# Array halves used in pairs, four pairs of weight halves for ten raw chunks: one change to a hybrid attention, scan and expert block

## The chip, the cores and the metric

The kernel runs on one core of one Trainium2 chip. The metric is the device time of one execution in microseconds; the kernel of before was run three times. An execution was also recorded by the hardware profiler, and every time that is shown here comes from the runs or from this record. In it PE is TensorE (matmul), PEld its weight loads, DVE VectorE, ACT ScalarE, POOL GpSimd and SP SyncE, which issues the weight transfers. L185 is line 185 of the kernel.

## The reference

512 tokens of width 1024 go through one block: modulation by a condition, a joint in-projection, attention in which an index score keeps 128 keys for each query, a Mamba2 scan beside it, a gated mix, and then 32 experts of which each token takes four.

```python
h = _rms(x, norm_mix[l]) * (1.0 + sc_m) + sh_m
q, kv_lat, q_i, k_i, w_i, z, xbc, dt_raw, gate_logits = _split(h @ w_in[l])
...
dots = jnp.einsum('bqhd,bsd->bqhs', qib, k_idx)              # index scores, 8 heads of 64
score = jnp.einsum('bqh,bqhs->bqs', wib, jax.nn.relu(dots))
_, sel = lax.top_k(score, topk)                              # 128 keys of a query
logits = jnp.einsum('bqhd,bqkhd->bqhk', qb, kg) * scale + bias   # 8 heads of 64
...
wmat = cb[..., None] * lmat * dtc[:, None]                   # scan: 16 heads of 64, chunks of 128
y = jnp.einsum('bijgh,bjghp->bighp', wmat, xc)
y = y + jnp.einsum('bign,bghpn->bighp', cc, state) * jnp.exp(acum)[..., None]
...
mixed = jax.nn.sigmoid(g_attn) * y_attn + jax.nn.sigmoid(g_ssd) * y_ssd
x = x + g_m * (mixed @ w_out[l])
h = _rms(x, norm_ffn[l]) * (1.0 + sc_f) + sh_f
...
gu = xb @ w_gu[e] + b_gu[e]                                  # expert e, blocks of 128 tokens
g, u = jnp.minimum(gu[:, :D_EXPERT], 7), jnp.clip(gu[:, D_EXPERT:], -7, 7)
out = ((u + 1.0) * (g * jax.nn.sigmoid(1.702 * g))) @ w_dn[e] + b_dn[e]
```

## The kernel before

**Weights.** Every weight chunk of 1 MB is loaded raw by SP's queue (`load` L176, `mload` L926) and split in two halves in the engine's rounded float type: the high half is a copy by ScalarE (`whi` L184, `mhi` L1297), the low half the rest, by VectorE (`wlo` L185, `mlo` L1298). TensorE then does three products, activations' high half by both and their low half by the weights' high half (L392 to L394 before the experts, L1338 to L1340 in them). In the experts a chunk is 12 matmuls of 128x512, and an expert is 12 chunks: four for gate and up (`gu`), two for down (`dn`), twice. The raw chunks go round a ring of buffers, RAW2 + 2 + RAW + RAW3 = 6 + 2 + 2 + 1 = 11; the halves go round HI + HI2 = 2 + 1 = 3 pairs (`msplit` L1283). A chunk's pair is asked for by `refill` (L1308) each time that `weights` hands one out, and EARLY = 3 of them are split before the first expert.

**Experts.** For gate and up, `gated` (L1267) lets ScalarE write silu into `g`, `upped` (L1271, L1272) has VectorE clip up into `u` and multiply into `act`. The activations are transposed on TensorE and split into `ah` (ScalarE, L1257) and `al` (VectorE, L1262), tokens likewise into `xh` and `xl` (L1259). `y` (L1368) is VectorE's eviction of `dn` with the gate. `si` (L1236) are the rows to which a block's result is scattered, and `put` (L1275) scatters it with a DMA. A scheduler decides the final order of each engine; it is pinned, so that an instruction that waits holds up all behind it.

**Before the experts.** A string, ORDER, says in which order the in-projection's pieces are written: c0 to c5 are the convolution's chunks, s1a to s3b index scores of four heads at 256, 384 and 512 keys (`scores`, L478), m is a piece of the modulation that VectorE computes. Then `weave` (L261) merges three stages by position: the scan with gate chunks and the top-128 search; attention with the z part; and the rest. In the scan, `ssd_terms` makes a head's two matrices (TensorE L752, L753, L759; then ScalarE's exponentials and VectorE's products), and `ssd_sum` adds up its output (L773, L775), one head at a time in 64 of the array's columns. In attention, `att_logits` makes one head's logits (L817, from 64 rows) and adds the mask (L818), VectorE adds a bias (L821), ScalarE takes the exponential; `att_sum` (L833 on) transposes and multiplies by the values.

Of the kernel before, what the change touches and what calls it, by code (L numbers as in the profile page):

```python
# [22 lines left out]
P = 128  # L23
# [110 lines left out]
def program(tc, A, dbg=None, upto=99):  # L134
# [5 lines left out]
    with ctx:  # L140
# [49 lines left out]
        RAW, HI, LO, RAW2, RAW3, HI2, R2, RAWP, EARLY = 2, 2, 2, 6, 1, 1, 6, 1, 3  # L190
        NS, ZEND, LATE, XFIRST = (4, 25, (0, 2, 3, 2.5), True)
# [9 lines left out]
        ORDER = "L S s1a R s1b m m s2a LT c0 K0 k0 m K1 VT c1 s2b m k1 Q0 c2 m c3 q0 s3a Q1 q1 s3b m m c4 m c5 m"  # L201
# [5 lines left out]
        with ExitStack() as c1:  # L207
# [264 lines left out]
            def scores(qt, hs):  # L472
                n = (qt + 1) * P
                sc = score[:, qt - 1, 0:n]
                for h in hs:
                    r = slice((h % 2) * 64, (h % 2) * 64 + 64)
                    p = pt("at")
                    T.matmul(p[:, 0:n], qiT[r, h // 2, qt * P:(qt + 1) * P], kiT[r, 0:n], start=True, stop=True)  # L478
                    rl = r2()
                    S.activation(rl[:, 0:n], p[:, 0:n], AF.Relu, scale=0.125)  # L480
                    if h == 0:
                        V.tensor_scalar(sc, rl[:, 0:n], wi8[:, qt, h:h + 1], None, op0=OP.mult)
                    else:
                        V.scalar_tensor_tensor(sc, rl[:, 0:n], wi8[:, qt, h:h + 1], sc, op0=OP.mult, op1=OP.add)
# [6 lines left out]
            dt_ = con.tile([P, NT, 16], F32, name="dt")  # L491
            acum, dec, expt = (con.tile([P, NT, 16], F32, name=n_) for n_ in ("acum", "dec", "expt"))
            hlt = []

            def steps():
# [185 lines left out]
            def vals():  # L681
                for t in range(NT):
# [10 lines left out]
                        s1a=lambda: scores(1, range(0, 4)), s1b=lambda: scores(1, range(4, 8)),  # L693
                        s2a=lambda: scores(2, range(0, 4)), s2b=lambda: scores(2, range(4, 8)),
                        s3a=lambda: scores(3, range(0, 4)), s3b=lambda: scores(3, range(4, 8)))
# [5 lines left out]
            bt, cT, hl = later["bt"], later["cT"], hlt[0]  # L701

# [44 lines left out]
            def ssd_terms(h):  # L747

                g = h // 8
                sel = selr[0:64, h:h + 1].to_broadcast([64, P])  # L750
# [3 lines left out]
                lm = r2((P, NT, P))  # L754
# [5 lines left out]
                ca = r2((P, 3 * P))  # L760
# [4 lines left out]
            def ssd_sum(h):  # L765
                g, a = h // 8, h % 2
                lm, ca = terms.pop(h)
                if a == 0:
                    terms["y"] = pt("sy")
                yp = terms["y"]  # L770
                for c in range(NT):
                    o = yp[a * 64:(a + 1) * 64, c * P:(c + 1) * P]
                    T.matmul(o, xdt[:, c, h * 64:(h + 1) * 64], lm[:, c, :], start=True, stop=(c == 0))  # L773
                    if c:
                        T.matmul(o, sts[:, slot[g][c - 1], (h % 8) * 64:(h % 8 + 1) * 64], ca[:, (c - 1) * P:c * P],  # L775
                                 start=False, stop=True)
                if a:
                    i = h // 2
                    V.scalar_tensor_tensor(yD[:, i, :], yD[:, i, :], dskip[:, i:i + 1], yp, op0=OP.mult, op1=OP.add)
# [15 lines left out]
            for g in range(2):  # L795
                scan += [lambda g=g, c=c: state(g, c) for c in range(3)]
                scan.append(lambda g=g: inner(g))
                for h in range(8 * g, 8 * g + 9):
                    scan += [lambda h=h: ssd_terms(h)] * (h < 8 * g + 8) + [lambda h=h: ssd_sum(h - 1)] * (h > 8 * g)
# [11 lines left out]
            def att_logits(qt, h):  # L811
                n = (qt + 1) * P
                if h == 0:
                    atts[qt] = pt("ac"), sm([P, 8], name="den")
                r = slice((h % 2) * 64, (h % 2) * 64 + 64)
                p = pt("at")
                T.matmul(p[:, 0:n], qT[r, h // 2, qt * P:(qt + 1) * P], kT[r, h // 2, 0:n], start=True, stop=False)  # L817
# [770 lines left out]
```

## Time and profile before

| what | value |
| --- | --- |
| time, median of 3 runs (range) | 1861.55 us (1860.41 to 1867.49) |
| time of the profiled execution, its span | 1862.16 us, 1860.3 us |
| TensorE busy, matmuls | 1783.4 us (96%), x8652 |
| VectorE busy | 1540.1 us (83%) |
| ScalarE busy | 1076.5 us (58%) |
| DMA, mean | 283 GB/s |

The span is the profiled time from the first instruction to the last. The shares are means over stages that differ: the parts before the experts take some 630 us, the experts the rest.

### The profile page before, as it was taken

The numbers are of one execution on the slowest core, as the hardware profiler recorded it, in microseconds if no ns is written. First come the engines' busy times: TensorE is split into PE (matmuls) and PEld (weight loads), VectorE is DVE, ScalarE is ACT, GpSimd is POOL, SyncE is SP. The second block draws the span as 40 slices with busy tenths as digits, with TensorE's granted clock in tenths as the row PEclk, the third lists the DMA queues.
The fourth block names the chain that finished last, engine by engine and source line by source line (L and its number), as shares of the span: only waits on it lengthen the run. The fifth ranks groups of instructions, "written<-read, shape, count | busy, mean of one in ns | idle before, by whom it ended". The sixth has DMA issues, their size and how long they took to land. (4 is left out here: it accounts for less than half of the span.)

```text
span 1860.3 us, 22834 instructions
## 1 busy us (share of the span) xinstructions
PE 1783.4 (96%) x8652; PEld 1400.4 (75%) x8652; DVE 1540.1 (83%) x1891; ACT 1076.5 (58%) x1059; POOL 191.9 (10%) x114
## 2 busy tenths in 40 slices
PE   7998999999999798999999999999999999999996
PEld 3777777776678577888888877777777777777875
DVE  6586787764776788999999899989899989988986
ACT  4453432344423365777777776766676667666764
POOL 0000000000000111101101101201111111210201
PEclk9999999999899799999999999999999999999998
DMA  8232343421575589999999999999999999999992
GB/s 324 91 139 89 114 161 123 144 105 69 187 264 210 198 276 352 371 369 369 390 375 374 365 363 373 361 367 355 382 358 347 384 381 340 361 384 354 369 345 56
DMA packets 86456, 527.26 MB, mean 283 GB/s; under 512 B 10912, under 2 KB 11072, under 8 KB 32072
## 3 DMA queue, kind: packets, MB, share of 16 engines
q1 hardware_dynamic: 70552, 469.70, 65.7%
q0 software_dynamic: 15552, 55.97, 11.1%
q8 instruction: 69, 1.13, 0.2%
q14 instruction: 43, 0.35, 0.1%
q10 hardware_dynamic: 240, 0.10, 0.0%
HBM read 497.91 MB, written 30.45 MB: 284 GB/s over the span
## 5 line engine op out<-in xcount | busy, mean ns | idle before, releaser
L185 DVE TENSOR_TENSOR wlo<-raw,whi 128x2048 fp32r<-128x2048 f32 x242 | 551.7, 2285 | 63.7 <-ACT whi L184 61.1
L184 ACT ACTIVATE whi<-raw 128x2048 fp32r<-128x2048 f32 x242 | 463.7, 1917 | 173.8 <-PE mm L393 73.4
L1297 ACT ACTIVATE mhi<-raw 128x2048 fp32r<-128x2048 f32 x104 | 199.7, 1921 | 86.4 <-PE gu L1340 74.0
L1298 DVE TENSOR_TENSOR mlo<-raw,mhi 128x2048 fp32r<-128x2048 f32 x104 | 237.4, 2283 | 1.8 <-ACT mhi L1297 1.8
L1339 PE MATMUL gu<-wlo,xh 128*128 128x512 f32 x520 | 209.4, 403 | 11.5 <-DVE wlo L185 11.4
L1339 PE MATMUL dn<-wlo,ah 128*128 128x512 f32 x508 | 205.3, 404 | 6.4 <-DVE wlo L185 5.4
L1338 PE MATMUL gu<-whi,xh 128*128 128x512 f32 x520 | 206.5, 397 | 0.0
L1340 PE MATMUL gu<-whi,xl 128*128 128x512 f32 x520 | 206.3, 397 | 0.0
L1340 PE MATMUL dn<-whi,al 128*128 128x512 f32 x508 | 201.2, 396 | 0.0
L1338 PE MATMUL dn<-whi,ah 128*128 128x512 f32 x508 | 199.7, 393 | 0.0
L1338 PE MATMUL gu<-mhi,xh 128*128 128x512 f32 x504 | 197.9, 393 | 1.4 <-ACT mhi L1297 1.4
L1339 PE MATMUL gu<-mlo,xh 128*128 128x512 f32 x504 | 198.3, 394 | 0.4 <-DVE mlo L1298 0.4
L1340 PE MATMUL gu<-mhi,xl 128*128 128x512 f32 x504 | 197.6, 392 | 0.0
L1275 POOL DMA_INDIRECT out_dram<-y,si x31 | 96.9, 3127 | 849.3 <-DVE y L1368 824.8
L393 PE MATMUL mm<-B,whi 128*128 128x512 f32 x352 | 140.1, 398 | 0.0
L392 PE MATMUL mm<-bA,whi 128*128 128x512 f32 x320 | 132.1, 413 | 3.8 <-ACT whi L184 1.8
L394 PE MATMUL mm<-bA,wlo 128*128 128x512 f32 x320 | 128.8, 404 | 4.2 <-DVE wlo L185 4.2
L1339 PEld LDWEIGHTS gu<-wlo,xh 128*128 128x128 f32 x520 | 98.0, 188 | 41.2 <-DVE wlo L185 21.6
L1339 PEld LDWEIGHTS dn<-wlo,ah 128*128 128x128 f32 x508 | 96.3, 190 | 35.8 <-DVE wlo L185 14.0
L1338 PEld LDWEIGHTS gu<-whi,xh 128*128 128x128 f32 x520 | 98.1, 189 | 22.0 <-ACT xh L1257 0.2
L1340 PEld LDWEIGHTS gu<-whi,xl 128*128 128x128 f32 x520 | 98.0, 188 | 20.8 <-DVE xl L1259 0.2
L1339 PEld LDWEIGHTS gu<-mlo,xh 128*128 128x128 f32 x504 | 95.0, 188 | 23.5 <-DVE mlo L1298 2.6
(453 smaller groups left out, 3122.7 us busy)
## 6 DMA issues: line engine op xcount, KB each, us to landing
raw<-in_w_gu_dram SPq DMA_DIRECT2D x209, 1024.0 KB
raw<-in_w_dn_dram SPq DMA_DIRECT2D x105, 1024.0 KB
B<-in_w_gu_dram SPq DMA_DIRECT2D x47, 1024.0 KB
raw<-in_w_in_dram SPq DMA_DIRECT2D x23, 1024.0 KB
B<-in_w_dn_dram SPq DMA_DIRECT2D x23, 1024.0 KB
rawp<-in_w_ada_dram POOLq DMA_DIRECT2D x30, 512.0 KB, 4.2
bE<-in_w_ada_dram SPq DMA_DIRECT2D x4, 1024.0 KB
bC<-in_x_dram SPq DMA_DIRECT2D x8, 512.0 KB
```

What stands on the lines that cost most here:

```text
L184: S.activation(hi[:, 0:n], raw[:, 0:n], AF.Copy)
L185: i = V.tensor_tensor(lo[:, 0:n], raw[:, 0:n], hi[:, 0:n].bitcast(F32), op=OP.subtract)
L392: T.matmul(p, wh, xT[0][:, k, :], start=(k == 0), stop=False)
L393: T.matmul(p, wh, xT[1][:, k, :], start=False, stop=False)
L394: T.matmul(p, wl, xT[0][:, k, :], start=False, stop=(k == nk - 1))
L1275: G.indirect_dma_start(out=out, out_offset=bass.IndirectOffsetOnAxis(ap=si, axis=0), in_=y, in_offset=None, compute_op=OP.add)
L1297: S.activation(hi, raw, AF.Copy)
L1298: i = V.tensor_tensor(lo, raw, hi.bitcast(F32), op=OP.subtract)
L1338: T.matmul(p, x[0][:, kk, :], hi[:, ws], start=(b is None and kk == 0), stop=False)
L1339: T.matmul(p, x[0][:, kk, :], lo[:, ws], start=False, stop=False)
L1340: T.matmul(p, x[1][:, kk, :], hi[:, ws], start=False, stop=(kk == KD - 1))
```

## The change

Index scores, logits, scan sums and attention sums are written for two heads at a time: both heads' matmuls stand next to each other in the code, each in its half of the array, and the steps that follow come behind. ORDER spreads the scores as pairs (s10 is the pair of heads 0 and 1 at 256 keys). The selector and `hl` of `ssd_terms` are widened from 64 to 128 rows, the new ones zero. The scan's and attention's temporaries get buffers of their own (`te`, six) beside `r2`. In the experts there are two pairs `mhi`/`mlo` (HI2 = 2), four pairs in all, and the eleventh raw chunk (`raw3`) goes; EARLY is 4; and ScalarE writes the gate straight into `act`, so `g` goes.

```diff
-        RAW, HI, LO, RAW2, RAW3, HI2, R2, RAWP, EARLY = 2, 2, 2, 6, 1, 1, 6, 1, 3
-        NS, ZEND, LATE, XFIRST = (4, 25, (0, 2, 3, 2.5), True)
+        RAW, HI, LO, RAW2, HI2, R2, RAWP, EARLY = 2, 2, 2, 6, 2, 6, 1, 4
+        NS, ZEND, LATE, XFIRST = (4, 13, (0, 2, 3, 2.5), True)
...
-        ORDER = "L S s1a R s1b m m s2a LT c0 K0 k0 m K1 VT c1 s2b m k1 Q0 c2 m c3 q0 s3a Q1 q1 s3b m m c4 m c5 m"
+        ORDER = "L S s10 R s12 m s14 m s16 LT s20 c0 s22 K0 k0 s24 m K1 VT s26 c1 m k1 s30 Q0 s32 c2 m s34 c3 q0 s36 Q1 q1 m m c4 m c5 m"
...
-                for h in hs:
-                    r = slice((h % 2) * 64, (h % 2) * 64 + 64)
-                    p = pt("at")
+                pair = [(h, slice((h % 2) * 64, (h % 2) * 64 + 64), pt("at")) for h in hs]
+                for h, r, p in pair:
                     T.matmul(p[:, 0:n], qiT[r, h // 2, qt * P:(qt + 1) * P], kiT[r, 0:n], start=True, stop=True)
+                for h, r, p in pair:
                     rl = r2()
...
-                hl = big("S8", [64, L], F32R)
+                hl = big("S8", [P, L], F32R)
                 hlt.append(hl)
-                S.activation(hl, pw[0:64, :], AF.Copy)
+                V.memset(hl[64:P].bitcast(F32), 0.0)
+                S.activation(hl[0:64], pw[0:64, :], AF.Copy)
...
-                sel = selr[0:64, h:h + 1].to_broadcast([64, P])
+                sel = selr[:, h:h + 1].to_broadcast([P, P])
...
-            def ssd_sum(h):
-                g, a = h // 8, h % 2
-                lm, ca = terms.pop(h)
-                if a == 0:
-                    terms["y"] = pt("sy")
-                yp = terms["y"]
+            def ssd_sum(i):
+
+                g = i // 4
+                two_ = [(h, slice((h % 2) * 64, (h % 2) * 64 + 64), *terms.pop(h)) for h in (2 * i, 2 * i + 1)]
+                yp = pt("sy")
                 for c in range(NT):
-                    o = yp[a * 64:(a + 1) * 64, c * P:(c + 1) * P]
-                    T.matmul(o, xdt[:, c, h * 64:(h + 1) * 64], lm[:, c, :], start=True, stop=(c == 0))
-                    if c:
-                        T.matmul(o, sts[:, slot[g][c - 1], (h % 8) * 64:(h % 8 + 1) * 64], ca[:, (c - 1) * P:c * P],
-                                 start=False, stop=True)
...
+                    cs = slice(c * P, (c + 1) * P)
+                    for h, r, lm, ca in two_:
+                        T.matmul(yp[r, cs], xdt[:, c, h * 64:(h + 1) * 64], lm[:, c, :], start=True, stop=(c == 0))
+                    for h, r, lm, ca in two_ if c else ():
+                        T.matmul(yp[r, cs], sts[:, slot[g][c - 1], (h % 8) * 64:(h % 8 + 1) * 64],
+                                 ca[:, (c - 1) * P:c * P], start=False, stop=True)
...
+                pair = [(h, slice((h % 2) * 64, (h % 2) * 64 + 64), pt("at")) for h in (h0, h0 + 1)]
+                for h, r, p in pair:
+                    T.matmul(p[:, 0:n], qT[r, h // 2, qt * P:(qt + 1) * P], kT[r, h // 2, 0:n], start=True, stop=False)
+                for h, r, p in pair:
+                    T.matmul(p[:, 0:n], identb, mask[:, qt - 1, 0:n] if qt else cmb, start=False, stop=True)
+                for h, r, p in pair:
+                    weighed(qt, h, n, p)
...
-                i = turn[0] % (RAW2 + 2 + RAW + RAW3)
+                i = turn[0] % (RAW2 + 2 + RAW)
...
-            def gated(g, p):
-                S.activation(g, p, AF.Silu, scale=ALPHA)
-
-            def upped(u, p, g, act):
+            def gated(act, p):
+                S.activation(act, p, AF.Silu, scale=ALPHA)
+
+            def upped(u, p, act):
 
                 V.tensor_scalar(u, p, 8.0, -6.0, op0=OP.min, op1=OP.max)
-                V.scalar_tensor_tensor(act, g, SILU7, u, op0=OP.min, op1=OP.mult)
+                V.scalar_tensor_tensor(act, act, SILU7, u, op0=OP.min, op1=OP.mult)
```

Where instructions come to stand is decided by the scheduler. On TensorE in the scan, the first head terms and sums of one group read before as follows (`ss` is a PSUM tile of the terms, `sy` the sums' one; `r_2152` and `r_2160` are one head's two matrices, and rows that read alike are counted behind the x).

```order
L752 MATMUL ss<-cmt,identb 128x512
L753 MATMUL ss<-bS_758,selr 128x512
L759 MATMUL ss<-bS_758,selr 128x384
L773 MATMUL sy<-r_2152,bC 64x128 x2
L775 MATMUL sy<-r_2160,bV 64x128
L773 MATMUL sy<-r_2152,bC 64x128
L775 MATMUL sy<-r_2160,bV 64x128
L773 MATMUL sy<-r_2152,bC 64x128
L775 MATMUL sy<-r_2160,bV 64x128
```

The same place in the changed kernel, where a sum begins behind a head's terms:

```order
L755 MATMUL ss<-cmt,identb 128x512
L756 MATMUL ss<-bS_758,selr 128x512
L762 MATMUL ss<-bS_758,selr 128x384
L776 MATMUL sy<-te,bC 64x128 x4
L778 MATMUL sy<-te,bV 64x128 x2
L776 MATMUL sy<-te,bC 64x128 x2
L778 MATMUL sy<-te,bV 64x128 x2
L776 MATMUL sy<-te,bC 64x128 x2
L778 MATMUL sy<-te,bV 64x128 x2
```

Seven groups of one head have become seven steps in which two heads alternate; a `sy` row counts both.

On VectorE in an expert of the later half (about the eighteenth), before:

```order
L1298 TENSOR_TENSOR mlo<-raw_9639,mhi 128x2048
L185 TENSOR_TENSOR wlo<-raw_9657,whi 128x2048
L1271 TENSOR_SCALAR u<-gu 128x512
L1272 SCALAR_TENSOR_TENSOR act<-g,u 128x512
L185 TENSOR_TENSOR wlo<-raw_9707,whi 128x2048
L1298 TENSOR_TENSOR mlo<-B_9725,mhi 128x2048
L1368 SCALAR_TENSOR_TENSOR y<-dn,gate,gf 128x512
L1262 SCALAR_TENSOR_TENSOR al<-tr,ah 128x512
L185 TENSOR_TENSOR wlo<-B_9746,whi 128x2048
L185 TENSOR_TENSOR wlo<-raw,whi 128x2048
L1298 TENSOR_TENSOR mlo<-raw,mhi 128x2048
L185 TENSOR_TENSOR wlo<-raw_9803,whi 128x2048
```

And the same stretch of the changed kernel:

```order
L1307 TENSOR_TENSOR mlo<-raw,mhi 128x2048
L185 TENSOR_TENSOR wlo<-raw_9680,whi 128x2048
L1280 TENSOR_SCALAR u<-gu 128x512
L1281 SCALAR_TENSOR_TENSOR act<-act,u 128x512
L185 TENSOR_TENSOR wlo<-raw_9698,whi 128x2048
L1307 TENSOR_TENSOR mlo<-raw_9719,mhi 128x2048
L1376 SCALAR_TENSOR_TENSOR y<-dn,gate,gf 128x512
L1271 SCALAR_TENSOR_TENSOR al<-tr,ah 128x512
L1307 TENSOR_TENSOR mlo<-raw_9737,mhi 128x2048
L185 TENSOR_TENSOR wlo<-raw_9758,whi 128x2048
L185 TENSOR_TENSOR wlo<-raw_9776,whi 128x2048
L1307 TENSOR_TENSOR mlo<-B_9808,mhi 128x2048
```

Between the splits, `u`, `act`, `y` and `al` stand where they stood; which splits are `wlo` and which `mlo` is now two and two in turn.

On VectorE at the start of the experts, ahead of the third place that writes `si`, before:

```order
L1467 TENSOR_TENSOR cum<-few 128x24
L1262 SCALAR_TENSOR_TENSOR al<-tr,ah 128x512
L1243 TENSOR_TENSOR gate<-q 128x4
L1466 COPY few<-cum 128x32
L1298 TENSOR_TENSOR mlo<-raw_5884,mhi 128x2048
L1244 TENSOR_TENSOR gate<-gate,q 128x4
L1467 TENSOR_TENSOR cum<-few 128x16
L185 TENSOR_TENSOR wlo<-raw_5902,whi 128x2048
L1236 TENSOR_TENSOR si<-q 128x4
L1468 CAST nbt<-cum 128x1
```

And in the changed kernel:

```order
L1376 SCALAR_TENSOR_TENSOR y<-dn,gate,gf 128x512
L1473 TENSOR_TENSOR cum<-few 128x24
L1271 SCALAR_TENSOR_TENSOR al<-tr,ah 128x512
L1252 TENSOR_TENSOR gate<-q 128x4
L1472 COPY few<-cum 128x32
L185 TENSOR_TENSOR wlo<-raw_5969,whi 128x2048
L1253 TENSOR_TENSOR gate<-gate,q 128x4
L1473 TENSOR_TENSOR cum<-few 128x16
L185 TENSOR_TENSOR wlo<-raw_5987,whi 128x2048
L1245 TENSOR_TENSOR si<-q 128x4
L1474 CAST nbt<-cum 128x1
```

Counted from the first expert on, one split more stands ahead of this `si` now.

## Rows read from the trace of the kernel before

**Rows 1.** Busy time by stretch: per engine us and instructions, TensorE clock, DMA share, GB/s.
```profile
245.00:377.00 132.00, 131.98 (x643) 95.37 (x641) 101.49 (x221) 47.55 (x105) 4.77 (x9) 1.00 0.41 147
245.00:265.00 20.00, 20.00 (x94) 13.66 (x93) 18.66 (x46) 9.70 (x24) 1.59 (x3) 1.00 0.47 165
377.00:448.00 71.00, 70.34 (x346) 50.04 (x345) 41.91 (x121) 31.23 (x82) 2.12 (x4) 1.00 0.22 75
762.00:1104.00 342.00, 342.00 (x1620) 278.92 (x1619) 318.26 (x233) 245.68 (x171) 46.32 (x19) 1.00 1.00 373
1104.00:1820.00 716.00, 703.93 (x3271) 562.47 (x3270) 648.70 (x480) 496.98 (x343) 99.45 (x36) 1.00 0.98 363
```

**Rows 2.** Waits from 1100 to 1800: who waited for whom, us, times, longest.
```profile
DVE u L1271 <- PE gu L1340: 33.5, 34, 1.0
...
DVE wlo L185 <- ACT whi L184: 14.3, 15, 1.0
...
PE gu L1339 <- DVE wlo L185: 10.1, 18, 0.7
...
SPq L942 <- DVE wlo L185: 356.4, 118, 4.2
SPq L942 <- DVE mlo L1298: 117.9, 59, 3.1
```

**Rows 3.** Timeline of VectorE and TensorE in one late expert: start, us, instruction.
```profile
1257.40 0.75 DVE L1368 SCALAR_TENSOR_TENSOR y<-dn,gate,gf 128x512 f32<-128x512 f32 x1 [0.69 <-PE dn L1340]
...
1258.66 4.48 DVE L185 TENSOR_TENSOR wlo<-raw,whi 128x2048 fp32r<-128x2048 f32 x2
...
1261.00 0.50 PE L1339 MATMUL gu<-wlo,xh 128*128 128x512 f32 x1 [0.66 <-DVE wlo L185]
```

**Rows 4.** Timeline of TensorE in the scan.
```profile
257.10 0.39 PE L752 MATMUL ss<-cmt,identb 128*128 128x512 bf16 x1
...
258.02 0.65 PE L773 MATMUL sy<-r,bC 128*64 128x128 f32 x4
...
259.70 0.50 PE L392 MATMUL mm<-bA,whi 128*128 128x512 f32 x1
260.03 0.39 PE L393 MATMUL mm<-B,whi 128*128 128x512 f32 x1
260.26 0.39 PE L394 MATMUL mm<-bA,wlo 128*128 128x512 f32 x1
...
297.90 0.65 PE L773 MATMUL sy<-r,bC 128*64 128x128 f32 x4
...
299.63 0.50 PE L392 MATMUL mm<-bA,whi 128*128 128x512 f32 x1
```

**Rows 5.** Timeline of TensorE, index scores of one and of two heads.
```profile
81.80 0.70 PE L478 MATMUL at<-bK,bV 64*128 64x256 f32 x4
...
88.12 0.70 PE L478 MATMUL at<-bK,bV 64*128 64x256 f32 x2
...
192.42 1.61 PE L478 MATMUL at<-bK,bV 64*128 64x512 f32 x4
...
199.90 1.12 PE L478 MATMUL at<-bK,bV 64*128 64x512 f32 x2
```

**Rows 6.** Timeline of TensorE, logits of one head.
```profile
423.33 0.91 PE L817 MATMUL at<-bE 64*128 64x384 f32 x2
424.18 0.34 PE L818 MATMUL at<-mask,identb 128*128 128x384 bf16 x1
```

**Rows 7.** Timeline of VectorE and TensorE at the start of the experts.
```profile
737.06 0.16 DVE L1236 TENSOR_TENSOR si<-q 128x4 int32<-128x4 f32 x1 [5.98 <-DMA out_dram<-y,si]
...
739.54 0.79 PE L1339 MATMUL dn<-wlo,ah 128*128 128x512 f32 x1 [4.85 <-DVE wlo L185]
```

**Rows 8.** Timeline of TensorE in the in-projection.
```profile
156.53 0.80 PE L394 MATMUL mm<-bA,wlo 128*128 128x512 f32 x1 [4.24 <-DVE wlo L185]
```

**Rows 9.** Waits from 762 to 1100.
```profile
ACT whi L184 <- DMA raw<-in_w_gu_dram: 4.9, 6, 0.9
```

More of the change, by code (lines that the diff above doesn't have):

```diff
@@ L490, in program @@
             na = con.tile([P, 16], F32, name="na")
[L491 to L492 removed]
+            dt_ = W.tile([P, NT, 16], F32, name="dt")
+            acum, dec, expt = (W.tile([P, NT, 16], F32, name=n_) for n_ in ("acum", "dec", "expt"))
             hlt = []
@@ L692, in program @@
                         q0=lambda: head_T(env["Q0"], 0, 0), q1=lambda: head_T(env["Q1"], 0, 2), m=mod_step,
-                        s1a=lambda: scores(1, range(0, 4)), s1b=lambda: scores(1, range(4, 8)),
-                        s2a=lambda: scores(2, range(0, 4)), s2b=lambda: scores(2, range(4, 8)),
-                        s3a=lambda: scores(3, range(0, 4)), s3b=lambda: scores(3, range(4, 8)))
+                        )
+            acts.update({f"s{qt}{h}": lambda qt=qt, h=h: scores(qt, (h, h + 1)) for qt in range(1, NT) for h in range(0, 8, 2)})
             acts.update({f"c{i}": lambda i=i: conv(i) for i in range(6)})
@@ L797, in program @@
                 scan.append(lambda g=g: inner(g))
-                for h in range(8 * g, 8 * g + 9):
-                    scan += [lambda h=h: ssd_terms(h)] * (h < 8 * g + 8) + [lambda h=h: ssd_sum(h - 1)] * (h > 8 * g)
+                for h in range(8 * g, 8 * g + 8):
+                    scan.append(lambda h=h: ssd_terms(h))
+                    if h % 2 == 0 and h > 8 * g:
+                        scan.append(lambda h=h: ssd_sum(h // 2 - 1))
+                scan.append(lambda g=g: ssd_sum(4 * g + 3))
             tops = [lambda qt=qt, i=i: top8(qt, i) for qt in range(1, NT) for i in range(16)]
@@ L896, in program @@
             yhi = big("C", [P, KD, L], F32R)
-            heads_ = [(qt, h) for qt in range(NT) for h in range(8)]
+            heads_ = [(qt, h) for qt in range(NT) for h in range(0, 8, 2)]
             steps_ = []
             for i in range(len(heads_) + 1):
-                steps_.append(lambda i=i: (att_logits(*heads_[i]) if i < len(heads_) else None, att_sum(*heads_[i - 1]) if i else None))
+                steps_.append(lambda i=i: (att_logits(*heads_[i]) if i < len(heads_) else None,
+                                           att_sum(*heads_[i - 1]) if i else None))
             zs = [lambda j=j, b=b: z_part(j, b) for j in range(4) for b in range(2)]
@@ L923, in program, with mload @@
             turn = [0, 0]
-            ahead, side = [], []
-            def mload(queue=nc.sync, tile_=None):
+            ahead = []
+            def mload():
                 src = next(order, None)
@@ L936, in mload @@
                         pool, name, n = M1, "raw2", RAW2
-                    elif i < RAW2 + 2:
+                    else:
                         pool, name, n = WB, f"B{i - RAW2}", 1
-                    else:
-                        pool, name, n = side[0], "raw3", RAW3
-                    raw = tile_ or pool.tile([P, 2048], F32, name=name, tag=name, bufs=n)
-                    i = queue.dma_start(raw, src)
-                    if queue is G:
-                        tc.keep_in_program_order(i)
+                    raw = pool.tile([P, 2048], F32, name=name, tag=name, bufs=n)
+                    nc.sync.dma_start(raw, src)
                 ahead.append(raw)
@@ L1435, in program @@
                     if e < NE:
-                        g, u = mt([P, 512], name="g", bufs=1), mt([P, 512], name="u", bufs=1)
-                        gated(g, three(xT, bias["b_gu"], e, f * 512, "gu", 3))
+                        u = mt([P, 512], name="u", bufs=1)
+                        gated(act[:, fs], three(xT, bias["b_gu"], e, f * 512, "gu", 3))
                         if e + f == 0:
@@ L1444, in program @@
                             held.extend("no")
-                        upped(u, three(xT, bias["b_gu"], e, FE + f * 512, "gu", 3), g, act[:, fs])
+                        upped(u, three(xT, bias["b_gu"], e, FE + f * 512, "gu", 3), act[:, fs])
                         if last:
```

58 lines of the change are left out of this document (28 added, 30 removed).

## The prediction

> **What bounds the kernel now.** I read the summary by engine first, then a table of busy times by stretch, then the waits of the engine that binds, and last the single instructions where the diff works. TensorE binds: in four of the five stretches of [rows 1] it is busy for practically the whole time, so that in them a microsecond taken off TensorE is a microsecond off the span as long as the other engines keep up. VectorE is close behind: 101.49 of 132 us in the stretch of the scan (245 to 377), 18.66 of 20 at its beginning, 318.26 of 342 in the early experts. That is the margin against which every gain below has to hold.
>
> The expert stage is in two regimes. In 762 to 1104 TensorE issues 1620 matmuls in 342 us, 4.737 per us; in 1104 to 1820 it issues 3271 in 716 us, 4.568 per us [rows 1]. At the first rate the second stretch would take 3271 / 4.737 = 690.5 us, so 25.5 us are lost there. [Rows 2] say on what: TensorE waits for wlo, the low half that VectorE makes of a weight chunk, and VectorE waits 33.5 us, 34 times, for TensorE to finish the group that `u` reads. Instructions show how one causes the other [rows 3]: VectorE stands at `y` until TensorE has finished dn, then does `y` and `al`, and only at 1258.66 begins the next low half; TensorE's first matmul with it starts at 1261.00. The pinned order lets VectorE be only one split ahead when it meets `y` or `u`; these two instructions and a split (1.26 us from 1257.40 to 1258.66, then half of the 4.48 us of two splits) take 3.5 us, longer than the 2.7 us for which TensorE can use the chunk it holds (12 matmuls at 0.23, the step of [rows 4] between 260.03 and 260.26). Transfers bind nothing here: the queue that issues them waits 356.4 + 117.9 us of this 700 us for VectorE to release a raw buffer [rows 2].
>
> **The change, part by part.** The sum is made against the profiled execution's own 1862.2 us (span 1860.3); the median of the runs is 1861.55, 0.6 less, which I neglect.
>
> *Index scores (L478).* A head fills half the rows of the array. Two heads on different halves take 0.70 us in 81.80, as long as a lone head in 88.12; at 512 columns a lone head takes 1.12 in 199.90 and a pair whose second head came late 1.61 in 192.42 [rows 5]. The step to the next matmul is some 0.07 shorter than such a row (0.85 against 0.91 in [rows 6]), so 0.63 and 1.05. In the order before, 18 heads stand in pairs and 6 alone, two of each length; now 4 pairs at 256 columns, 3 pairs and 2 lone heads at 384, and at 512 two pairs, three heads in a row and one alone. Fewer clusters: 5 x 0.63 becomes 4 x 0.63 at 256, nothing at 384, between 0 and 0.5 at 512, together 0.6 to 1.1. Lateness like that of 192.42 (0.5 us) is in several pairs of before, and the new code asks for both results before the first matmul. I take 2 us, from 0.6 to 4.
>
> *Scan sums (now L776, L778).* A head uses 64 of the array's columns. Alone it takes 1.68 us for its 14 matmuls (258.02 to 259.70). From 297.90, 18 matmuls take 1.73: four of the next head's stand among the last of the first and cost 0.05 us [rows 4]. If each of the 16 heads ran beside another, 8 x 1.68 = 13.4 us would go. The order shows that the new sums do stand interleaved, two by two. But it breaks 5 of the 8 pairs after the first group or two, and the pieces pay entry and exit. From 0 to 13, I take 8: below the full overlap, above half of it.
>
> *Scan terms.* The three matmuls with the 64-row selector take 0.92 us from 257.10 to 258.02. At the 0.23 of a full step, with 3/4 of it for the third, they would be 0.63 [rows 4]. The selector now has all 128 rows, so a head can lose 0.29 and 16 heads 4.6 us. I take 4.5, since both bounds lie near each other; the zeros for it cost one small memset.
>
> Together 12.5 us of TensorE in the scan. It does not all reach the span: with it gone, VectorE would have 101.49 us of work in 119.5, and in 245 to 265, where it had 1.34 us free, TensorE can't gain more than that. I count nine tenths, **-11**, with 0 and -17 as ends.
>
> *Attention logits (L821).* Before, no two heads' products stood together. One at 384 columns takes 0.85 us (423.33 to 424.18) [rows 6]; the score rows give 0.63 at 256 and 1.05 at 512, and the step between them 0.42 at 128. In the new order 2 of 4 pairs stand together at 128, all 4 at 256, 3 at 384 and only 1 at 512: 0.84 + 2.52 + 2.55 + 1.05 = 7.0 us. TensorE is busy 70.34 of 71 us in the larger part of this stage [rows 1]; the 512-column heads partly lie behind it, where it waits anyway. I take **-6**, from -2 to -9.
>
> *Fourth pair of halves, in steady experts.* This is the largest question: 25.5 us could come back. The order says not. From the twelfth expert on, `u`, `act`, `y` and `al` stand at the same places between splits as before (the steady expert shown above), and VectorE again meets `u` and `y` with one split in hand. A free pair doesn't help an engine whose next instruction is pinned behind `y`. ScalarE may make high halves earlier, but the time lost is in VectorE's queue. I take 0, with -25 as the bound. In experts 2 to 9 VectorE is now one split further ahead, but TensorE lost nothing there. The order falls back to one split ahead some one and a half experts sooner: 25.5 us over 19 experts is 1.3 each, so **+2**.
>
> *Start of the experts.* Writing `si` makes VectorE wait 5.98 us for a transfer, and TensorE stands until 739.54, 4.85 us, for the split behind it [rows 7]. In the new order one more split stands ahead of `si`: 12 matmuls, 2.7 us, with which TensorE fills this wait. Its first steps afterwards are long (0.79 us for the first), and a shorter stop may spare some of them. I take **-3**, from 0 to -5.
>
> *Everything else.* One raw buffer fewer costs nothing while the transfers wait for VectorE, as they do for over two thirds of the time in [rows 2]. The gate written into act's place removes a buffer, no instruction. The stall before 156.53 (4.24 us behind a chain of small norms on VectorE) [rows 8] goes, since its split now stands ahead of the chain, but the split after it has moved behind; I take 0, from -4 to +4. The tail keeps its order.
>
> Sum: -2 -11 -6 +0 +2 -3 = -20, so 1862.2 - 20 = **1842 us**; with the terms' own bounds, not all at once at their ends, 1828 to 1853.
>
> **The rivals.** *B, the fourth pair heals the experts.* If VectorE's waits for ScalarE's high halves, 14.3 us in 15 [rows 2], are what keeps it from getting ahead, a pair more would remove them, and the later experts would run at the early rate: -25, so 1817 us. Against it: the same single split of lead in the pinned order. For it: the early experts, on the same number of pairs, do run with more lead.
>
> *C, TensorE's gain in phase 1 is not realised.* Paired sums ask VectorE and ScalarE for two heads' terms at once. VectorE at 18.66 of 20 us can't deliver faster, and TensorE would then wait for `lm` and `ca`. Scan and attention together would give 4 instead of 17: 1862.2 - 2 - 4 + 2 - 3 = 1855 us. In the worst case, with nothing from either, 1859. The Trainium skill (TensorEngine Tiling (Array Packing), section PSUM Bottleneck) says just this of packing: the array gets faster, evacuating PSUM doesn't, and the copy may become the limit. By that rule the sum would be C's; the trace agrees for the first 20 us of the scan and, with VectorE at 77% of 245 to 377, not for the whole.
>
> *D, ten raw chunks are too few* (slower). A raw buffer is held from the issue of its transfer to the end of its split. A chunk is 12 matmuls, at least 12 / 4.568 = 2.6 us [rows 1], so eleven buffers give each 29 us for this and ten 26. Where issue, landing and split need more than those 26 us, the transfers set the pace. If they needed the full 29, the 1058 us of experts from 762 to 1820 would grow by a tenth, +106, and with the -19 of phase 1 the time would be about 1949; from a fifth of that on, the kernel is slower than before. For it: the DMA share of 1.00 and 0.98 [rows 1], and ScalarE's six waits for a transfer in the early experts, 4.9 us in all [rows 9]. Against it: these waits reach no matmul, no engine waits for a weight transfer later, and the issuing queue itself waits for a buffer over two thirds of the time [rows 2].
>
> **How the numbers follow.** 0.5% of this kernel, about 9.3 us, is what a measurement can tell from no change. Forecast 0.63 (1828 to 1853), B 0.10 (1817), C 0.19 (1853 to 1859), D 0.05 (above 1872), other 0.03. Faster: 0.61 of the forecast, B, and 0.07 of C, 0.78. Same: 0.02 + 0.11 of C + 0.02 = 0.15; slower: D and part of the rest, 0.07. A range from 1816 to 1860 takes in B and C and leaves out D and what lies beyond.
>
> **What would show it.** The scan and attention stretch: TensorE's sums in pairs, 28 matmuls in about 1.7 to 2.2 us, terms in 0.65 us, and the experts' first matmuls some 18 us earlier. In the later experts the same 10 us of TensorE waits for wlo and the same rate of 4.57 matmuls per us. `si` with a TensorE wait of some 2 us instead of 4.85. I would be wrong if the later experts run at 4.7 (B), if TensorE waits in 245 to 377 for `te` (C), or if ScalarE waits for raw transfers (D).

## The result and the profile after

The changed kernel takes **1845.99 us** (median of 5 runs, 1842.02 to 1848.25) against 1861.55 (5 runs, 1859.01 to 1867.49): ratio 0.9911, interval 0.9888 to 0.9933. The forecast was 1842, with a range of 1816 to 1860. The execution that was profiled is the slowest of the five (1848.25 us, span 1846.5), so sums made from its rows come out 2 us short of the medians.

Where did the time go? The simplest way to see it is a ledger of landmarks: instructions that both kernels have once, at the borders of the stages, and the difference of their starts. First the timeline of TensorE in the kernel before: the scan's first state, its last term, the router, the first expert matmul, then the 37th, 145th and 373rd weight chunk of the experts (in experts 3, 12 and 31 of 0 to 31), and the last matmul.

```profile
237.62 0.59 PE L729 MATMUL ss<-r,bF 128*128 128x512 f32 x1
...
368.00 0.44 PE L759 MATMUL ss<-bS,selr 64*128 64x384 f32 x1
...
592.48 0.19 PE L1170 MATMUL mm<-bfc,bK 128*32 128x1 f32 x1
...
646.90 0.79 PE L1338 MATMUL gu<-whi,xh 128*128 128x512 f32 x1
...
774.23 0.39 PE L1338 MATMUL dn<-whi,ah 128*128 128x512 f32 x1
...
1100.97 0.39 PE L1338 MATMUL dn<-whi,ah 128*128 128x512 f32 x1
...
1811.07 0.39 PE L1338 MATMUL dn<-whi,ah 128*128 128x512 f32 x1
...
1847.01 0.40 PE L1340 MATMUL dn<-whi,al 128*128 128x512 f32 x1
```

The same eight in the changed kernel:

```profile
245.25 0.59 PE L732 MATMUL ss<-r,bF 128*128 128x512 f32 x1
...
360.40 0.38 PE L762 MATMUL ss<-bS,selr 128*128 128x384 f32 x1
...
577.58 0.19 PE L1179 MATMUL mm<-bfc,bK 128*32 128x1 f32 x1
...
631.13 0.79 PE L1346 MATMUL gu<-whi,xh 128*128 128x512 f32 x1
...
754.79 0.39 PE L1346 MATMUL dn<-whi,ah 128*128 128x512 f32 x1
...
1083.77 0.39 PE L1346 MATMUL dn<-whi,ah 128*128 128x512 f32 x1
...
1797.10 0.39 PE L1346 MATMUL dn<-whi,ah 128*128 128x512 f32 x1
...
1833.69 0.40 PE L1348 MATMUL dn<-whi,al 128*128 128x512 f32 x1
```

The differences are +7.6, -7.6, -14.9, -15.8, -19.4, -17.2, -14.0 and -13.3 us. A difference that stays is a stage that costs the same; one that changes is a gain or a loss made between two landmarks. Both kernels' first score stands 0.6 apart (82.42 after 81.80 in [rows 5]), so the stages read:

| stage | forecast, us | measured, us |
| --- | --- | --- |
| in-projection with scores, to the scan's first state | -2 | +7.0 |
| scan, to its last term | -11 | -15.2 |
| attention and out-projection | -6 | -7.3 |
| router and gather | 0 | -0.9 |
| start of the experts, to expert 3 | -3 | -3.7 |
| experts 3 to 12 | +2 | +2.2 |
| experts 12 to 31 | 0 | +3.2 |
| tail | 0 | +0.7 |

Five stages came within 1.3 us of the forecast. The scan gave 4.2 us more, and two stages lost time that was not forecast: the in-projection and experts 12 to 31. The rows behind what came as forecast: TensorE in the scan, a head's terms and the sum of two heads (columns as in [rows 4]).

```profile
293.23 0.39 PE L755 MATMUL ss<-cmt,identb 128*128 128x512 bf16 x1
...
293.96 0.66 PE L776 MATMUL sy<-te,bC 128*64 128x128 f32 x8
...
295.64 0.51 PE L392 MATMUL mm<-bA,whi 128*128 128x512 f32 x1
```

The terms take 0.73 us where they took 0.92 in [rows 4]; the sum is 28 matmuls in 1.68 us (293.96 to 295.64), the time that 14 took for one head. In this sum the overlap is whole. VectorE is busy for 115.41 of 132 us in 245 to 377, against 101.49 in [rows 1]. TensorE waits for it there twice, 0.5 us each; one of the two is the wait for `te` that the prediction named as a sign of rival C:

```profile
PE sy L776 <- DVE te L760: 0.5, 1, 0.5
```

TensorE with two heads' logits:

```profile
392.55 0.70 PE L821 MATMUL at<-bE 64*128 64x256 f32 x4
393.18 0.39 PE L823 MATMUL at<-mask,identb 128*128 128x256 bf16 x2
```

Two heads at 256 columns take 0.63 us, as forecast for a pair. At the start of the experts, VectorE and TensorE at `si` (compare [rows 7]):

```profile
721.58 0.16 DVE L1245 TENSOR_TENSOR si<-q 128x4 int32<-128x4 f32 x1 [4.99 <-DMA out_dram<-y,si]
...
724.06 0.72 PE L1347 MATMUL gu<-mlo,xh 128*128 128x512 f32 x1 [2.55 <-DVE mlo L1307]
```

`si` waits nearly as long as before, but TensorE's wait behind it shrinks from 4.85 to 2.55 us by the one more split. And in the later experts, TensorE's waits between 1100 and 1800 (columns as in [rows 2]):

```profile
PE gu L1347 <- DVE mlo L1307: 8.7, 13, 0.7
PE dn L1347 <- DVE wlo L185: 3.1, 4, 0.8
PE gu L1347 <- DVE wlo L185: 0.6, 1, 0.6
```

18 waits and 12.4 us in all, where [rows 2] have 18 and 10.1: the fourth pair took none of them away.

In the stage that went wrong, TensorE shows two new stops of over 1.5 us, one ahead of the matmuls for `dt`'s running sum and one at a pair of scores:

```profile
101.12 0.43 PE L521 MATMUL ac<-da,cst 128*128 128x64 f32 x2 [1.73 <-DVE da L516]
...
171.18 2.07 PE L477 MATMUL at<-bK,bV 64*128 64x512 f32 x2 [3.37 <-ACT r L480]
```

After both, single matmuls of 128x512 take 0.63 to 0.80 us instead of 0.39 for a while. The table by stretch, from 100 to 125 us, for the kernel before and then the changed one (columns as in [rows 1]; the third number from the right is the clock):

```profile
100.00:125.00 25.00, 23.10 (x134) 17.89 (x134) 21.45 (x45) 14.04 (x32) 1.31 (x2) 1.00 0.47 174
```

```profile
100.00:125.00 25.00, 23.67 (x104) 16.26 (x105) 18.11 (x39) 11.67 (x28) 0.81 (x2) 0.80 0.51 191
```

TensorE is as busy as before and does 104 instructions instead of 134: it is at half clock, the lower of its two levels, for part of the stretch. Busy time alone would have hidden this. The same over the whole stage, before and then changed:

```profile
82.00:245.00 163.00, 154.83 (x789) 118.36 (x788) 124.10 (x254) 70.58 (x119) 4.49 (x8) 0.98 0.33 117
```

```profile
82.00:245.00 163.00, 154.52 (x762) 117.17 (x761) 117.45 (x242) 67.79 (x116) 4.21 (x8) 0.93 0.31 107
```

TensorE's idle time is nearly the same, 8.2 and 8.5 us; the clock is not. As an estimate, 0.05 of 163 us is 8 us, which is about the 7.0 us of the table.

### The profile page after: what moved, and what is told of

Its sections match the earlier page's. It is cut to its first block, busy times and chain, and to the rows that moved or that the text cites. A ratio compares the mean times of both kernels' runs of the same rounds, so it can differ in the third digit from the quotient of the medians.

```text
span 1846.5 us, 22809 instructions
## 1 busy us (share of the span) xinstructions
PE 1769.5 (96%) x8652; PEld 1393.0 (75%) x8652; DVE 1537.6 (83%) x1892; ACT 1056.2 (57%) x1059; POOL 186.2 (10%) x114
## 5 line engine op out<-in xcount | busy, mean ns | idle before, releaser
L185 DVE TENSOR_TENSOR wlo<-raw,whi 128x2048 fp32r<-128x2048 f32 x188 | 428.2, 2286 | 35.6 <-ACT whi L184 33.9
L184 ACT ACTIVATE whi<-raw 128x2048 fp32r<-128x2048 f32 x188 | 355.5, 1911 | 120.8 <-PE mm L393 75.6
L1307 DVE TENSOR_TENSOR mlo<-raw,mhi 128x2048 fp32r<-128x2048 f32 x152 | 346.8, 2285 | 16.3 <-ACT mhi L1306 15.9
L1306 ACT ACTIVATE mhi<-raw 128x2048 fp32r<-128x2048 f32 x152 | 288.8, 1915 | 39.1 <-PE gu L1348 25.0
L1347 PE MATMUL gu<-mlo,xh 128*128 128x512 f32 x512 | 205.3, 401 | 13.3 <-DVE mlo L1307 13.3
L1347 PE MATMUL gu<-wlo,xh 128*128 128x512 f32 x512 | 203.6, 398 | 0.6 <-DVE wlo L185 0.6
L1266 ACT ACTIVATE ah<-tr 128x512 fp32r<-128x512 f32 x64 | 38.1, 595 | 160.8 <-PE tr L1265 160.5
L1346 PEld LDWEIGHTS gu<-mhi,xh 128*128 128x128 f32 x512 | 96.8, 189 | 20.7
L1348 PEld LDWEIGHTS gu<-mhi,xl 128*128 128x128 f32 x512 | 96.7, 189 | 19.8
L1347 PE MATMUL dn<-wlo,ah 128*128 128x512 f32 x264 | 106.4, 403 | 4.4 <-DVE wlo L185 3.4
```

Source lines behind the costliest of these rows:

```text
L184: S.activation(hi[:, 0:n], raw[:, 0:n], AF.Copy)
L185: i = V.tensor_tensor(lo[:, 0:n], raw[:, 0:n], hi[:, 0:n].bitcast(F32), op=OP.subtract)
L1266: S.activation(hi[:, 4 * b:4 * b + 4, :], p, AF.Copy, scale=scale)
L1306: S.activation(hi, raw, AF.Copy)
L1307: i = V.tensor_tensor(lo, raw, hi.bitcast(F32), op=OP.subtract)
L1346: T.matmul(p, x[0][:, kk, :], hi[:, ws], start=(b is None and kk == 0), stop=False)
```

## Experiments

Each kernel below was timed in five rounds beside the kernel before on the same chip; ratios are to that. That kernel's median was 1861.5 to 1862.6 us in these groups, so differences of about 1 us between kernels of different groups say nothing.

**Phase 1 alone.** The expert stage is put back.

```diff
-        RAW, HI, LO, RAW2, HI2, R2, RAWP, EARLY = 2, 2, 2, 6, 2, 6, 1, 4
+        RAW, HI, LO, RAW2, RAW3, HI2, R2, RAWP, EARLY = 2, 2, 2, 6, 1, 1, 6, 1, 3
...
-                i = turn[0] % (RAW2 + 2 + RAW)
+                i = turn[0] % (RAW2 + 2 + RAW + RAW3)
```

> The changed kernel with its expert stage put back: three pairs, eleven raw chunks, the gate in its own buffer; all pairing before the experts stays. My theory, that the whole gain of the change was made before the experts (the first expert matmul 15.8 us earlier) and that the experts gave 2 us back: 1862 - 16 = 1846 us or 1 to 2 less than the changed kernel, later experts at the rate of before. Rival, that the fourth pair is worth something which a loss elsewhere hides (the start of the experts gained 3.7 us): 1849 to 1850, slower than the changed kernel.

Measured: 1846.73 us, ratio 0.9919 (0.9897 to 0.9941), the changed kernel's time within 1 us, as the theory expected; its rival asked for 1849 to 1850.

**The experts' part alone**, in the kernel before:

```diff
-        RAW, HI, LO, RAW2, RAW3, HI2, R2, RAWP, EARLY = 2, 2, 2, 6, 1, 1, 6, 1, 3
+        RAW, HI, LO, RAW2, HI2, R2, RAWP, EARLY = 2, 2, 2, 6, 2, 6, 1, 4
...
-            dt_ = con.tile([P, NT, 16], F32, name="dt")
+            dt_ = W.tile([P, NT, 16], F32, name="dt")
```

> The kernel before with the expert part of the change alone: four pairs, ten raw chunks, the gate in act's place (and the four small tables dt, acum, dec, expt in the other pool, which makes the room). My theory, that u and y meet one split of lead whatever the number of pairs: no change, 1860 to 1865 us, with the start of the experts 3 to 4 us shorter and the later experts 0.1 to 0.2 us longer each. Rival B, that a fourth pair heals the experts: 1837 us. Rival D, that ten raw chunks hold the experts up: above 1870 us and waits of ScalarE for raw chunks.

Measured: 1861.16 us, ratio 0.9998 (0.9985 to 1.001). Four pairs with ten raw chunks are worth nothing in sum: what the start gains is given back later. In this run's profile the start, to expert 3, is 7.4 us shorter than in the kernel before, and the two stages behind it, to expert 12 and to expert 31, are 2.2 and 2.9 us longer. B and D both fall, and no engine waits for a raw chunk between 1100 and 1800 in the changed kernel.

**Scores as before.** `scores` goes head by head again, and ORDER is the old string.

```diff
-        ORDER = "L S s10 R s12 m s14 m s16 LT s20 c0 s22 K0 k0 s24 m K1 VT s26 c1 m k1 s30 Q0 s32 c2 m s34 c3 q0 s36 Q1 q1 m m c4 m c5 m"
+        ORDER = "L S s1a R s1b m m s2a LT c0 K0 k0 m K1 VT c1 s2b m k1 Q0 c2 m c3 q0 s3a Q1 q1 s3b m m c4 m c5 m"
```

> The changed kernel with the index scores as before: groups of four heads, one head after the other, and the old order of the in-projection's pieces. My theory, that the scan's start came 7.0 us later than forecast because the scores' new places in the order make TensorE stop for ScalarE (3.37 us before 171.18) and run at a low clock after it: the 7 us come back, 1838 to 1840 us, and the granted clock of 100 to 245 is again near 0.98 instead of 0.92. Rival, that other parts of the change (tables in another pool, the wider hl) cost this time: 1846 us as it is.

Measured: 1850.36 us, ratio 0.9928 (0.9905 to 0.9952). The theory on record before this run fell: the scan's first state stands at 245.29, where it stood in the changed kernel.

**Old order, paired scores.**

```diff
-        ORDER = "L S s10 R s12 m s14 m s16 LT s20 c0 s22 K0 k0 s24 m K1 VT s26 c1 m k1 s30 Q0 s32 c2 m s34 c3 q0 s36 Q1 q1 m m c4 m c5 m"
+        ORDER = "L S s10 s12 R s14 s16 m m s20 s22 LT c0 K0 k0 m K1 VT c1 s24 s26 m k1 Q0 c2 m c3 q0 s30 s32 Q1 q1 s34 s36 m m c4 m c5 m"
```

> The changed kernel with the scores in pairs, but these at the old places in the order of pieces (two pairs where a group of four heads stood). If the places cost the 7 us: 1837 to 1840 us, a little better than with the scores wholly undone, since pairs take fewer clusters. If the pairing itself does it (two results asked for before the first is evicted): 1845 to 1848 us.

Measured: 1847.96 us, ratio 0.9921 (0.99 to 0.9942), scan at 245.11. Neither the places nor the pairing, then, or not these alone. What all four kernels with a late scan share is the wider `hl`, whose new rows are cleared on VectorE. In the order that the scheduler makes, the clear stands where a weight split stood, and splits and convolution steps behind it change places. VectorE in the kernel before and then in the changed one:

```profile
84.60 2.29 DVE L185 TENSOR_TENSOR wlo<-raw,whi 128x2048 fp32r<-128x2048 f32 x1
```

```profile
85.47 0.48 DVE L532 MEMSET bS<- 64x512 f32 x1 [0.16 <-issue]
...
95.45 2.29 DVE L185 TENSOR_TENSOR wlo<-raw,whi 128x2048 fp32r<-128x2048 f32 x1
```

The clear takes 0.48 us, and the split comes some 10 us later.

**The clear on GpSimd.**

```diff
-                V.memset(hl[64:P].bitcast(F32), 0.0)
+                G.memset(hl[64:P].bitcast(F32), 0.0)
```

> The changed kernel with the one clear of the 64 new rows of hl on GpSimd instead of VectorE. New theory, since undoing the scores did not bring the 7 us back and the scan began at 245 us in all four kernels that have the wider hl: the clear on VectorE moves the order of the in-projection behind it (a split and convolution steps change places), which costs TensorE stops and a low clock. Then the scan begins 6 to 7 us earlier, about 239, and the time is 1838 to 1841 us. Rival, that the scores' new places cost the time by themselves: 1845 to 1848 us, scan at 245.

Measured: 1843.68 us, ratio 0.9890 (0.9873 to 0.9906); the scan begins at 242.19. That is 3.1 us earlier than in the changed kernel, about half of what I expected:

```profile
242.19 1.88 PE L732 MATMUL ss<-r,bF 128*128 128x512 f32 x4
```

The 2.3 us between the two medians are no more than the spread of the runs; the earlier start is the firmer reading.

**The same, with the scores and ORDER as before.**

> The changed kernel with the scores and the order of pieces as before, and the clear on GpSimd. VectorE's order is then that of the kernel before up to the scan. If the clear is the cause of the late scan: scan at 238 to 239 us, 1842 to 1844 us, 7 less than with the scores undone alone (1850). If something else that these kernels share is (the tables in the other pool, the te buffers): 1848 to 1851 us and scan at 245.

Measured: 1840.52 us, ratio 0.9875 (0.9857 to 0.9893), the best so far, and 9.8 less than with the clear on VectorE. The first states of the scan, in the timeline of TensorE with the scores undone, and then with the clear on GpSimd as well:

```profile
245.29 1.88 PE L733 MATMUL ss<-r,bF 128*128 128x512 f32 x4
```

```profile
240.40 1.88 PE L733 MATMUL ss<-r,bF 128*128 128x512 f32 x4
```

So the scan begins 4.9 us earlier because one small instruction moved to another engine. The rest of the 9.8 lies in the stage behind 445 us, where the clock is 0.50 between 460 and 475 in the one profile and 1.00 in the other; that part differs between executions of like programs (last section).

**The clear alone**, added to the kernel before. The selector goes on reading 64 rows.

```diff
-                hl = big("S8", [64, L], F32R)
+                hl = big("S8", [P, L], F32R)
...
-                S.activation(hl, pw[0:64, :], AF.Copy)
+                V.memset(hl[64:P].bitcast(F32), 0.0)
+                S.activation(hl[0:64], pw[0:64, :], AF.Copy)
```

> The kernel before with one thing added: hl made 128 rows tall and its 64 new rows cleared on VectorE; the selector still reads 64 rows, so no product changes. If the clear's place in VectorE's order is what made the scan late: 1866 to 1871 us, scan's first state at 242 to 245 instead of 238, and a low clock for a stretch after 100 us. Rival, that the clear costs only its own 0.3 us and matters only together with the other edits: 1860 to 1864 us.

Measured: 1873.5 us (7 runs, 1865.77 to 1875.22), ratio 1.0042 (1.0022 to 1.0061). Slower, as the theory has it; the median lies above the range expected, and the runs spread widely. The stretch from 100 to 125 us and the scan's first state in this kernel:

```profile
100.00:125.00 25.00, 23.09 (x117) 17.36 (x116) 19.54 (x43) 11.48 (x24) 0.73 (x1) 0.86 0.57 205
```

```profile
245.02 1.88 PE L730 MATMUL ss<-r,bF 128*128 128x512 f32 x4
```

The clock is 0.86 where it was 1.00, and the scan begins 7.4 us later than in the kernel before. The other edits aren't needed for it.

Over all the profiles, the time from the first score to the scan's first state separates the two parts (us, with the number of kernels):

| | scores and ORDER as before | new ORDER |
| --- | --- | --- |
| no clear on VectorE | 155.5 to 156.5 (4) | 159.9 to 160.1 (2) |
| clear on VectorE | 161.8 to 162.2 (2) | 161.1 to 162.8 (5) |

Paired scores at the old places, with the clear on VectorE, take 161.7. Each part alone makes this stage late, the clear by 5 to 7 us and the new code and places of the scores by 3 to 5; together they cost hardly more than the clear.

**The selector on 64 rows as before**, which needs no clear.

```diff
-                sel = selr[:, h:h + 1].to_broadcast([P, P])
+                sel = selr[0:64, h:h + 1].to_broadcast([64, P])
...
-                hl = big("S8", [P, L], F32R)
+                hl = big("S8", [64, L], F32R)
```

> The changed kernel with hl and the selector on 64 rows as before, so with no clear at all; VectorE's order before the scan is that of the kernel with the clear on GpSimd. If the clear's place is the cause: 4 to 5 us more than that kernel, 1843 to 1845 us, for 16 heads at 0.29 us in the terms, and the scan begins at the same time as there. Rival, that half-row products cost nothing beside others: the same time as that kernel. Rival, that the clear has no part in it: 1850 us, the changed kernel plus 4.6.

Measured: 1852.07 us, ratio 0.9937 (0.9922 to 0.9951), 8.4 more than with the clear on GpSimd instead of 4 to 5. The scan itself, from its first state to its last term, is 115.4 us with the clear on GpSimd (242.19 to 357.62) and 120.3 with 64 rows (243.38 to 363.70), so 4.9, close to the forecast of 16 x 0.29 = 4.6. The scan's first state in this kernel:

```profile
243.38 1.88 PE L731 MATMUL ss<-r,bF 128*128 128x512 f32 x4
```

TensorE's last term in the one and the other:

```profile
357.62 0.37 PE L762 MATMUL ss<-bS,selr 128*128 128x384 f32 x1
```

```profile
363.70 0.43 PE L761 MATMUL ss<-bS,selr 64*128 64x384 f32 x1
```

Of the other 3.5 us, 1.2 lie ahead of the scan and the rest behind it. Their cause is not known.

**Sums head by head.** The joint step stays, the matmuls of the second head stand behind those of the first.

```diff
-                for c in range(NT):
-                    cs = slice(c * P, (c + 1) * P)
-                    for h, r, lm, ca in two_:
+                for h, r, lm, ca in two_:
+                    for c in range(NT):
+                        cs = slice(c * P, (c + 1) * P)
```

> The changed kernel with the scan's sums written head by head again inside the new joint step, nothing else changed. My theory, that two heads overlap only where their matmuls alternate in the order: the sums take some 26 us instead of 16, the scan's last term is 8 to 10 us later against its first state, 1853 to 1856 us. Rival, that the scan gains from fewer interruptions or from the buffers of its own (te) and not from the overlap: 1845 to 1848 us.

Measured: 1856.3 us, ratio 0.997 (0.9955 to 0.9984), 10.3 more than the changed kernel. First state and last term:

```profile
244.72 1.88 PE L732 MATMUL ss<-r,bF 128*128 128x512 f32 x4
...
368.75 0.34 PE L762 MATMUL ss<-bS,selr 128*128 128x384 f32 x1
```

The scan takes 124.0 us here, 115.2 in the changed kernel (245.25 to 360.40) and 130.4 before (237.62 to 368.00): 8.9 of its 15.2 us are had only by letting the two heads' matmuls alternate. One sum shows it directly:

```profile
296.53 0.43 PE L776 MATMUL sy<-te,bC 128*64 128x128 f32 x2
...
299.14 0.39 PE L755 MATMUL ss<-cmt,identb 128*128 128x512 bf16 x1
```

Here 26 of the 28 matmuls of two heads take 2.61 us (two stand ahead by themselves), where all 28 take 1.68 when they alternate. It isn't twice 1.68, since at the seam the last matmuls of one head run beside the first of the next, as in [rows 4].

**A longer lead for VectorE.** In the changed kernel, from the ninth expert on, `u` and `y` are tied behind the splits that stand ahead of them in the code.

```diff
-                V.tensor_scalar(u, p, 8.0, -6.0, op0=OP.min, op1=OP.max)
+                i = V.tensor_scalar(u, p, 8.0, -6.0, op0=OP.min, op1=OP.max)
+                if turn[1] > LEAD:
+                    tc.keep_in_program_order(i)
...
-                V.scalar_tensor_tensor(y[:, ns], p, info[e][2], gf[:, ns], op0=OP.mult, op1=OP.mult)
+                i = V.scalar_tensor_tensor(y[:, ns], p, info[e][2], gf[:, ns], op0=OP.mult, op1=OP.mult)
+                if LEAD < turn[1] < 12 * NE - 12:
+                    tc.keep_in_program_order(i)
```

> The changed kernel with u and y tied, from the ninth expert on, behind the splits that stand ahead of them in the code, so that VectorE meets u with three more splits done (212 instead of 209 splits before the same u). My theory, that the 25 us of the later experts are lost to the single split of lead: the later experts run at 4.73 matmuls per us as the early ones do, TensorE's 10 to 12 us of waits for low halves vanish, 1822 to 1828 us. Rival, that VectorE, the transfers or the ten raw buffers set the later rate: 1844 to 1848 us with new waits on VectorE for ScalarE or on ScalarE for raw chunks.

Measured: **1821.94 us**, ratio 0.9777 (0.9761 to 0.9793). The stretch from 1104 to 1780 and the waits of TensorE and VectorE in it; the changed kernel's stretch stands behind:

```profile
1104.00:1780.00 676.00, 670.76 (x3172) 546.59 (x3171) 624.05 (x466) 473.33 (x333) 68.72 (x36) 1.00 0.99 372
...
PE dn L1350 <- DVE wlo L185: 5.2, 4, 1.3
...
DVE wlo L185 <- ACT whi L184: 26.4, 14, 2.5
DVE hot L1005 <- PE dn L1234: 15.2, 4, 3.8
```

```profile
1104.00:1780.00 676.00, 663.23 (x3090) 530.73 (x3089) 612.26 (x457) 452.74 (x324) 95.32 (x35) 1.00 0.98 363
```

3172 matmuls instead of 3090 in the same 676 us, 4.69 per us. All waits of `gu` for low halves are gone. What is left, 5.2 us in four waits, stands where VectorE waits for `hot`, once in four experts.

**The same lead on three pairs**, that is in the kernel of the first experiment.

> The kernel with the pairing before the experts, the expert stage of before (three pairs, eleven raw chunks), and u and y tied behind the splits ahead of them as in the run with four pairs (211 splits before the same u instead of 209, one less than there). If the lead alone decides and three pairs hold it: the same 1822 to 1826 us. If the fourth pair is what lets VectorE use the lead, because with three a split has to wait for a pair that TensorE still reads: 1830 us or more, with waits of ScalarE and VectorE for pairs in the later experts.

Measured: 1827.23 us, ratio 0.9815 (0.9796 to 0.9835), between the two expectations. The same stretch:

```profile
1104.00:1780.00 676.00, 671.76 (x3172) 546.24 (x3171) 627.88 (x467) 484.34 (x333) 66.03 (x36) 1.00 1.00 372
...
PE gu L1355 <- DVE mlo L1314: 3.9, 4, 1.0
...
ACT whi L184 <- PE dn L1356: 61.7, 74, 1.0
```

The rate is the same, 3172 matmuls. ScalarE does wait for pairs (61.7 us for `dn` alone), but this reaches TensorE for 3.9 us at most. The 5 us between the two medians are matched by the start: from the first expert matmul to expert 3 it is 121.2 us with four pairs (636.8 to 757.9) and 126.5 with three (632.0 to 758.5). From there to the last matmul three pairs are 1.1 us faster.

**What proved useful, together**: pairing in scan and attention, 128-row terms, the old scores and ORDER, the clear on GpSimd, four pairs, the lead.

> The pieces that proved useful together: pairing in the scan and in attention, terms on 128 rows, scores and order of pieces as before, the clear on GpSimd, four pairs of halves, and u and y tied behind the splits ahead of them. If the gains add: 1840.5 - 24 = 1815 to 1818 us, below every other kernel here. If the lead's gain shrinks because the experts start elsewhere: 1820 to 1824 us.

Measured: **1818.02 us** (1814.31 to 1822.36), ratio 0.9757 (0.9739 to 0.9776): 28 us below the changed kernel, and at the upper end of what was expected if the gains add. The lead's 24 us came as 22.5.

## Why the prediction came out right, and where not

*TensorE binds, and pairs of heads take half the time.* Right. The scan gave 15.2 us for 11: the sums gave 8.9 by experiment for 8, the terms 4.9 for 4.5, and the discount to nine tenths for VectorE's sake was not needed. The remaining 1.4 of the 15.2 I can't assign. Attention gave 7.3 for 6, with its stretch to the router. No run undoes the pairing in attention by itself, and this stretch differs by some 4 us between profiles: it is 217.1 to 221.5 us in the eleven kernels with pairs and 222.9 to 229.8 in the three without. The means differ by the same 7.3, but the share of the pairing is argued, not shown.

*Rival C, that VectorE or the evictions eat the gain.* Wrong in the scan: VectorE went to 87% of that stretch, and TensorE stayed at 130.95 of 132 us, with the one wait of 0.5 us for `te`. The Trainium skill (TensorEngine Tiling (Array Packing), section PSUM Bottleneck) says that the copy out of PSUM may become the bottleneck after a fourfold speedup of TensorE; at a packing of two it did not here.

*Fourth pair.* Right in the main: no gain in steady experts, the start -3.7 for -3, the earlier fall to a short lead +2.2 for +2. The start varies: it takes 119.7 to 123.9 us in the ten profiles with four pairs and 125.9 to 127.3 in the four with three. The cause was argued from the order at first; the two runs with a longer lead show it, since with three pairs and with four the rate rises alike, and with a short lead it doesn't. Not foreseen are the 3.2 us that experts 12 to 31 lost; the forecast had 0. TensorE's waits for low halves grew by 2.3 us, with a row of four `dn` waits, 3.1 us in all, that the kernel before doesn't have. The stretch takes 713.0 to 713.6 us in the eight kernels with four pairs and a short lead, the experts' part alone among them, and 710.1 to 710.7 in the three with three pairs. So it belongs to the experts' part; which of its edits does it is open.

*The step that failed* is the one on everything else: "the zeros for it cost one small memset", and the stall in the in-projection "I take 0". The clear costs its place in VectorE's order: 0.48 us of work put a split some 10 us later. On GpSimd instead, the scan begins 3 us earlier in the new order of scores and 5 in the old. The scores' new places are the second part: with the clear on GpSimd, first score to first state is 159.9 us in the new order (82.3 to 242.2) and 156.5 in the old (83.9 to 240.4; 155.8 before). The forecast had -2 for the scores; by this pair of runs they cost 3.4, and with the clear on VectorE about nothing more. The stall behind the norms did go (4.24 us before 156.53, with a low clock after it), and a shorter one for a split came, as written (0.80 us before 179.11); but the two stops shown above, 1.73 and 3.37 us with a low clock after each, were not in the forecast.

*The sum* was right partly by luck, because errors met: 9 us too hopeful before the scan, 5.5 too careful in the scan and attention, 3 too hopeful in the later experts.

## What to carry to other kernels

Where engines wait for each other in a pinned order, count by how many steps the feeding engine is ahead when it meets an instruction that waits; here more buffers bought nothing in sum while the order didn't use them, and two tied instructions gave more than the whole change. Small matmuls that use half of the array's columns gave most of their gain only when they alternated in the order; for halves of the rows this was not tried. An instruction of half a microsecond can cost many times that by its place: after a change, compare landmarks stage by stage, with the clock and the count of instructions beside the busy time.

## What the runs showed of the hardware

The low clock after a stop of TensorE lasts for different times in executions of like programs. After the stop near 440 us (2.42 us in both) the clock is half for some 20 us in the changed kernel's profile, and for 30 in that of the longer lead, whose code is the same up to there. First the changed kernel, then the other, with columns as in [rows 1]:

```profile
445.00:460.00 15.00, 15.00 (x59) 12.50 (x59) 5.06 (x22) 3.98 (x10) 0.53 (x1) 0.50 0.21 76
460.00:475.00 15.00, 14.86 (x80) 9.62 (x79) 11.24 (x31) 8.15 (x18) 0.53 (x1) 0.84 0.23 65
```

```profile
445.00:460.00 15.00, 15.00 (x60) 12.37 (x59) 5.62 (x23) 4.43 (x13) 0.53 (x1) 0.51 0.26 99
460.00:475.00 15.00, 15.00 (x45) 8.88 (x45) 8.24 (x22) 4.56 (x10) 0.53 (x1) 0.50 0.11 36
```

With 80 instructions against 45 in the second of these stretches, this is 4 to 5 us by itself: the router stands 217.2 us behind the scan's last term in the one (360.4 to 577.6) and 221.5 in the other (361.2 to 582.7). It is nearly as much as the spread of the five runs, and as the part of several differences above that I could not assign.
